# Expert gate and up weights in tiles of their own, one product each, and an unused product beside the routing: a two-block network on one Trainium2 core

## The chip, the cores and the metric

The kernel runs on one NeuronCore of a Trainium2 chip. The metric is the device time of one execution in microseconds (us). The engines are PE (TensorE; its weight loads are shown apart, as PEld), DVE (VectorE), ACT (ScalarE), POOL (GpSimd) and SP (SyncE, which here issues nearly all loads). An L with a number, such as L1540, is a line of the kernel.

## The reference

Two blocks are computed one after the other on 256 tokens of width 1024, all in float32: a recurrent and sliding-window block with an MLP, then a block with latent attention, pooling, attention to a memory, and a mixture of experts. The change lies in the mixture of experts, which ends the program:

```python
group_prob = softmax(xn @ w_rg + b_rg); g_w, g_idx = top_k(group_prob, 1)
sel = (the 8 expert logits of the chosen group)
e_w, e_idx = top_k(softmax(sel), 2)
cw = (g_w * renormalised e_w, spread over the 32 experts)
for e in range(32):
    hid = silu(xn @ w_gate[e]) * (xn @ w_up[e])       # 1024 x 256 each
    out = out + (hid * cw[:, e:e+1]) @ w_down[e]      # 256 x 1024
x = rms_norm(x + out, final_norm_g)
```

Each token goes to 2 of 32 experts, but all experts' weights are read: 32 x 3 matrices of 1 MB.

## The kernel before

The program is written in the order in which each engine is to do its work; that order is kept. Loads go out on SP's queue in one fixed list (`raws`), each as soon as a slot for it is free. A **raw** is 1 MB of weights. There are ten big slots (7 and 3), and up to eight small ones, each made of two half-size activation tiles (`rawa`).

**The experts' rounds.** After the routing the experts are put in order of their load and worked through in ten rounds: four wide rounds of two experts with 64 token slots each, then six rounds of four experts with 32 slots each. Two rounds make a batch. In a round the experts stand side by side: expert i's products write the output partitions from 64i (or 32i), so that their products run at the same time on different columns of the array. The first six experts have fixed numbers, so their 18 raws can be loaded before the routing is known and fill all 18 slots; later ones are looked up (`ids`).

**One expert's weights.** `load_gu` (L1438) fills one raw with half of the 1024 rows of gate and of up: four rows to a partition (runs of 4 KB in DRAM), gate in one half of the tile and up in the other, two DMAs. In a small slot the same takes four DMAs with runs of 2 KB. `load_d` (L1447) loads the down matrix in runs of 8 KB, or of 4 KB in a small slot. `gu` (L1533) multiplies: for each of four k of a half, one product of 512 columns gives gate and up at once (L1540). `first` (L1588) does this for the first half, `second` (L1604) for the second half and then the activation; `down` (L1597) transposes the hidden values, multiplies by the down matrix and adds the result of the round before to the output (`scatter`).

**The routing.** `after_x(c)` (L1066) runs when half c of the block's residual x is done: it transposes x for the logits (L1091), sums squares (L363, into the place of the split), and copies x into `xs[t][0]` on ACT (L1097). `fours` (L1101) is the order of these copies: four neighbouring columns of x are put 128 apart, so that tile k of the transposed x fits the weights' rows. `split_rest` (L1106) takes the remainder of that split on DVE (L1109). `prepare0` (L1520) then runs, in this order: `residual(0)` (L1573; a product with the identity that puts x into the output's accumulators, L1578), `route` (L1282, a chain of small DVE steps from L1291 to L1318, then five small PE products from L1321), `onehots(0)` (L1470, L1474), `places` (the experts' order), `gather(0, ...)` for k 0 to 3 (L1482: each k takes four products on PE, L1490, and a copy with the norm's gain on ACT, L1493), `split_rest(1)`, and `weights` (DVE steps up to `cws`, L280). The first round's `first` follows, and in it the other four gathers, `slots_of(0)` (L1494, which reads `cws`) and `residual(1)`. For later batches `second` runs the gathers of the next batch, four before its products and four after the activation.

Of the kernel before, what the change touches and what calls it, by code (L numbers as in the profile page):

```python
# [10 lines left out]
F32 = mybir.dt.float32  # L11
# [10 lines left out]
P = 128  # L22
# [77 lines left out]
class Net:  # L100
# [965 lines left out]
    def after_x(self, c):  # L1066
# [13 lines left out]
        sq = lambda t: self.sumsq(self.X[t][:, cs], 512, self.xs[t][0][:, cs])  # L1080
# [25 lines left out]
    def split_rest(self, c):  # L1106
        cs = slice(c * 512, (c + 1) * 512)
        for t in range(2):
            self.nc.vector.tensor_sub(self.fours(self.xs[t][1], c), self.X[t][:, cs],  # L1109
                                      self.fours(self.xs[t][0], c).bitcast(F32))  # L1110
# [134 lines left out]
    def setup3(self):  # L1245
# [12 lines left out]
        for n, d in ((slice(0, 4), slice(0, 4)), (slice(4, 36), slice(8, 40))):  # L1258
            nc.gpsimd.tensor_tensor(self.wr[:, :, d], w[:, :, n], g.to_broadcast([P, 8, n.stop - n.start]), op=ALU.mult)
            nc.gpsimd.tensor_copy(self.br[:, d], self.free[:, o + n.start:o + n.stop])  # L1260
        self.tri = cp.tile([P, P], BF16, name="tri")
# [20 lines left out]
    def route(self):  # L1282
# [36 lines left out]
        s2 = sel01.rearrange("p t g e -> p t (g e)")  # L1319
        p = self.pt((P, 3, E))  # L1320
# [4 lines left out]
        nc.tensor.matmul(p[:, 2, :], self.ones, s2[:, 1, :], start=False, stop=True)  # L1325
        self.pm = self.cp.tile([P, 2, E], F32, name="pm")
# [91 lines left out]
    def moe(self):  # L1418
# [38 lines left out]
        def gu_of(raw, k):  # L1457

            x = raw[k * len(raw) // 4].rearrange("p a b -> p (a b)").rearrange("p (j k n) -> p j k n", j=2, n=256)
            return x[:, :, k % (4 // len(raw)), :]  # L1460
# [21 lines left out]
        def gather(b, kts):  # L1482
            for k in kts:
# [9 lines left out]
                nc.scalar.mul(xg[b, k // 4][:, k % 4, :], p, self.col("ffn_cols", k, 1))  # L1493
# [26 lines left out]
        def prepare0():  # L1520
            self.small_slots = 16
            self._loads()
            residual(0)
# [251 lines left out]
```

## Time and profile before

| what | value |
|---|---|
| median of 3 runs | 966.74 us (965.71 to 968.67) |
| the profiled execution | 966.64 us, its span 964.9 us |
[...]
| PE busy / DVE / ACT | 904.4 / 547.6 / 472.5 us |
| bytes read from DRAM | 220.59 MB, 230 GB/s over the span |

The page also cuts the span into 40 slices of 24 us. These lines give, for each slice, the granted TensorE clock and the busy share of PE and of the DMA engines in tenths, and the GB/s that they moved:

```profile
PE   6999999999999999999999999999998999857775
PEclk9999999999999999999999999999997999879768
DMA  9644244586365555454665444356678999999994
GB/s 292 212 142 172 89 132 148 170 292 209 95 217 201 193 184 200 162 178 134 208 212 171 176 156 153 132 177 212 246 267 320 370 406 400 389 409 409 406 406 185
```

Such lines are read by stage: a digit of 9 tells which resource is full there. [...]

### The profile page before, as it was taken

To read this page: it belongs to the slowest core of one execution; us is meant where nothing else is said; L and a number is where in the kernel's file an instruction comes from. 1 tells how busy PE (TensorE), PEld (TensorE's weight loads), DVE (VectorE), ACT (ScalarE), POOL (GpSimd) and SP (SyncE) were. 2 spreads that over 40 slices of the span, in tenths; PEclk is the share of its full clock that TensorE was granted. 3 is DMA by queue.
4 is the path that set the end of the run, shared out by engine and by line. 5 is a ranking of instruction groups with operands and counts; after the bars stand their busy time and mean duration, and the time that the engine had idled before them with its cause. 6 is when DMAs were issued, how large, how long until landed. Compare 5 with 4: busy or idle time off the path is not lost.

```text
span 964.9 us, 14222 instructions
## 1 busy us (share of the span) xinstructions
PE 904.4 (94%) x5265; PEld 700.6 (73%) x5265; DVE 547.6 (57%) x1101; ACT 472.5 (49%) x900; POOL 34.6 (4%) x71
## 2 busy tenths in 40 slices
PE   6999999999999999999999999999998999857775
PEld 5889898888899999988988787999884444313212
DVE  5986889776675555567756558856447222201002
ACT  5666779754655454456665645645542322102002
POOL 4200000000000000000200000000000000000000
PEclk9999999999999999999999999999997999879768
DMA  9644244586365555454665444356678999999994
GB/s 292 212 142 172 89 132 148 170 292 209 95 217 201 193 184 200 162 178 134 208 212 171 176 156 153 132 177 212 246 267 320 370 406 400 389 409 409 406 406 185
DMA packets 97783, 222.63 MB, mean 231 GB/s; under 512 B 9378, under 2 KB 13739, under 8 KB 96427
## 3 DMA queue, kind: packets, MB, share of 16 engines
q1 hardware_dynamic: 94016, 218.91, 63.7%
q10 hardware_dynamic: 3691, 2.74, 0.9%
q8 instruction: 43, 0.70, 0.3%
q14 instruction: 33, 0.27, 0.1%
HBM read 220.59 MB, written 1.05 MB: 230 GB/s over the span
## 4 chain that ended last, share of the span: by engine, by line
PE 79%; DMA 14%; DVE 3%; issue 2%; ACT 1%; SPq 1%; POOL 0%; DVEq 0%; ACTq 0%; POOLq 0%
PE acc L313 18%; PE acc L315 18%; PE acc L314 18%; PE pt L1540 5%; DMA raw<-in_w_exp_gate_dram 4%; DMA rawa<-in_w_exp_down_dram 4%; PE pt L314 3%; PE pt L315 3%; PE pt L313 3%; DMA raw<-in_w_exp_up_dram 2%; DMA rawa<-in_w_exp_gate_dram 2%; PE pt L1562 2%; PE pt L286 1%; PE pt L1490 1%; DMA raw<-in_w_exp_down_dram 1%
## 5 line engine op out<-in xcount | busy, mean ns | idle before, releaser
L280 DVE TENSOR_TENSOR w<-raw,w 128x512 fp32r<-128x512 f32 (+4 forms) x288 | 273.5, 968 | 117.8 <-ACT w L279 115.9
L279 ACT CAST w<-raw 128x512 fp32r<-128x512 f32 (+4 forms) x288 | 236.4, 847 | 153.7 <-PE acc L315 117.8
L313 PE MATMUL acc<-w,st 128*128 128x512 f32 (+2 forms) x508 | 197.7, 392 | 0.0
L314 PE MATMUL acc<-w,st 128*128 128x512 f32 (+2 forms) x508 | 197.4, 389 | 0.0
L315 PE MATMUL acc<-w,st 128*128 128x512 f32 (+2 forms) x508 | 193.3, 389 | 0.2 <-DVE w L280 0.2
L1540 PE MATMUL pt<-raw,xg 128*32 128x512 f32 (+1 forms) x360 | 97.4, 698 | 31.3 <-DMA raw<-in_w_exp_up_dram 31.3
L315 PEld LDWEIGHTS acc<-w,st 128*128 128x128 f32 x508 | 95.8, 189 | 19.1 <-DVE w L280 0.6
L313 PEld LDWEIGHTS acc<-w,st 128*128 128x128 f32 x508 | 95.9, 189 | 18.4 <-ACT st L279 0.5
L314 PEld LDWEIGHTS acc<-w,st 128*128 128x128 f32 x508 | 96.0, 189 | 17.6 <-DVE st L280 0.2
L1540 PEld LDWEIGHTS pt<-raw,xg 128*32 128x32 f32 (+1 forms) x360 | 22.6, 131 | 86.8 <-issue 82.4
L280 DVE TENSOR_TENSOR y<-pt,y 128x512 fp32r<-128x512 f32 x20 | 13.8, 692 | 123.4 <-ACT y L279 123.4
L314 PE MATMUL pt<-st,w 128*128 128x256 f32 x256 | 73.1, 286 | 1.8 <-DVE w L280 1.8
L315 PE MATMUL acc<-st,w 128*128 128x256 f32 x256 | 73.7, 288 | 0.0
L313 PE MATMUL acc<-st,w 128*128 128x256 f32 x256 | 73.5, 287 | 0.0
L314 PE MATMUL acc<-st,w 128*128 128x256 f32 x256 | 73.4, 287 | 0.0
L313 PE MATMUL pt<-st,w 128*128 128x256 f32 x256 | 73.0, 286 | 0.0
L315 PE MATMUL pt<-st,w 128*128 128x256 f32 x256 | 72.5, 286 | 0.0
L314 PEld LDWEIGHTS pt<-st,w 128*128 128x128 f32 x256 | 49.9, 195 | 2.2 <-DVE w L280 2.0
L313 PE MATMUL acc<-w,hid 128*128 128x512 f32 x128 | 50.0, 390 | 0.0
L313 PEld LDWEIGHTS pt<-st,w 128*128 128x128 f32 x256 | 49.8, 195 | 0.2
L314 PE MATMUL acc<-w,hid 128*128 128x512 f32 x128 | 49.9, 390 | 0.0
L315 PE MATMUL acc<-w,hid 128*128 128x512 f32 x128 | 49.8, 389 | 0.0
(393 smaller groups left out, 1346.4 us busy)
## 6 DMA issues: line engine op xcount, KB each, us to landing
raw<-in_w_in_dram SPq DMA_DIRECT2D x31, 1024.0 KB, 5.2
raw<-in_w_exp_gate_dram SPq DMA_DIRECT2D x45, 512.0 KB, 7.0
raw<-in_w_exp_up_dram SPq DMA_DIRECT2D x45, 512.0 KB, 8.0
rawa<-in_w_exp_down_dram SPq DMA_DIRECT2D x44, 512.0 KB, 8.7
raw<-in_w_up_dram SPq DMA_DIRECT2D x16, 1024.0 KB, 5.6
raw<-in_w_down_dram SPq DMA_DIRECT2D x16, 1024.0 KB, 6.2
raw<-in_w_exp_down_dram SPq DMA_DIRECT2D x10, 1024.0 KB, 10.0
rawa<-in_w_exp_gate_dram SPq DMA_DIRECT2D x38, 256.0 KB, 7.5
```

Of the source, the lines that this page charges most:

```text
L279: self.nc.scalar.copy(h, src)
L280: self.nc.vector.tensor_sub(l, src, h.bitcast(F32))
L286: self.nc.tensor.transpose(p[:, i, :], src[:, i * P:(i + 1) * P], self.ident)
L313: mm(acc, xh, wh, start=start, stop=False)
L314: mm(acc, xl, wh, start=False, stop=False)
L315: mm(acc, xh, wl, start=False, stop=stop)
L1490: nc.tensor.matmul(p, xs[t][i][:, k * P:(k + 1) * P], oh[b, t], start=n == 0, stop=n == 3)
L1540: nc.tensor.matmul(guP[p][q].rearrange("s (j f) -> s j f", j=2), xg[b, hf][:, k, j * P + q.start:j * P + q.stop], gu_of(x, k), start=kt == ...
L1562: nc.tensor.matmul(q[s], hT[p][:, f, s], d_of(x, f, c), start=f == 0, stop=f == 1)
```

## The change

`load_m` replaces `load_gu`: a raw now holds one whole matrix of an expert, gate or up, with eight rows to a partition, in one DMA (two in a small slot). `first` multiplies by gate alone and `second` by up alone, each with eight products of 256 columns. The order of x's columns follows (`eights` in place of `fours`, and the gain `g8`, loaded by a small DMA on ACT's queue). All eight gathers are now needed before `first`. The remainder of x's second half is taken in two parts: for tokens 0 to 127 at the end of `after_x(1)`, for the others after `onehots(0)`. `keep` issues products into an accumulator that is overwritten later: ten ahead of the routing's PE products and four behind them. The four accumulators are taken at the start of `prepare0`. (A path for overfull experts, which does not run with these inputs, changes likewise.)

```diff
@@ after_x
-        sq = lambda t: self.sumsq(self.X[t][:, cs], 512, self.xs[t][0][:, cs])
+        sq = lambda t: self.sumsq(self.X[t][:, cs], 512)
...
         for t in range(2):
-            nc.scalar.copy(self.fours(self.xs[t][0], c), self.X[t][:, cs])
-        if c == 0:
-            self.split_rest(0)
+            nc.scalar.copy(self.eights(self.xs[t][0], c), self.X[t][:, cs].rearrange("q (p k) -> q p k", k=8))
+        for t in range(2 - c):
+            self.split_rest(c, t)
-    def fours(self, x, c):
-        return x[:, c * 512:(c + 1) * 512].rearrange("q (k p) -> q p k", k=4)
+    def eights(self, x, c):
+        return x.rearrange("q (k p) -> q p k", k=8)[:, c * 64:(c + 1) * 64, :]
...
+    def keep(self, acc, n):
+        for _ in range(n):
+            self.nc.tensor.matmul(acc, self.identr, self.eights(self.xs[0][0], 0), start=True, stop=True)
@@ setup3
+        self.g8 = cp.tile([P, 8], F32, name="g8")
...
+        nc.scalar.dma_start(self.g8, rows.rearrange("(p k) -> p k", k=8))
@@ route
+        self.keep(self.acc[0, 1], 10)
         p = self.pt((P, 3, E))
         nc.tensor.matmul(p[:, 0, :], self.tri, s2[:, 0, :], start=True, stop=True)
...
         nc.tensor.matmul(p[:, 2, :], self.ones, s2[:, 1, :], start=False, stop=True)
+        self.keep(self.acc[0, 1], 4)
@@ moe
-        def load_gu(e, hf):
+        def load_m(e, w):
             def f(parts):
-                n = 4 // len(parts) * 256
+                rows = e.of(w).rearrange("(p k) n -> p (k n)", k=8)
+                n = 2048 // len(parts)
                 for i, x in enumerate(parts):
-                    for j, w in enumerate((wg, wu)):
-                        rows = e.of(w)[hf * 512:(hf + 1) * 512, :].rearrange("(p k) n -> p (k n)", k=4)
-                        runs = x.rearrange("p a b -> p (a b)")
-                        nc.sync.dma_start(runs[:, j * n:(j + 1) * n], rows[:, i * n:(i + 1) * n])
+                    nc.sync.dma_start(x.rearrange("p a b -> p (a b)"), rows[:, i * n:(i + 1) * n])
...
         def prepare0():
...
+            for t in range(2):
+                for c in range(2):
+                    acc[t, c] = self.accp()
             residual(0)
             places, weights = self.route()
             onehots(0)
+            self.split_rest(1, 1)
             places()
-            gather(0, range(4))
-            self.split_rest(1)
+            gather(0, range(8))
             weights()
...
-        def gu(p, hf, tiles):
+        def gu(p, i, tiles):
...
-            for k in range(4):
-                kt = 4 * hf + k
+            for k in range(8):
                 for x, q in zip(tiles, own(p)):
-                    nc.tensor.matmul(guP[p][q].rearrange("s (j f) -> s j f", j=2),
-                                     xg[b, hf][:, k, j * P + q.start:j * P + q.stop], gu_of(x, k), start=kt == 0,
-                                     stop=kt == 7)
+                    nc.tensor.matmul(guP[p][q, i * 256:(i + 1) * 256],
+                                     xg[b, k // 4][:, k % 4, j * P + q.start:j * P + q.stop], m_of(x, k), start=k == 0,
+                                     stop=k == 7)
...
-        gus = [[[load_gu(e, hf) for e in of_round(p)] for hf in range(2)] for p in range(NP)]
+        gus = [[[load_m(e, w) for e in of_round(p)] for w in (wg, wu)] for p in range(NP)]
...
             if p == 0:
-                gather(0, range(4, 8))
                 slots_of(0)
                 residual(1)
...
         def second(p, tiles):
             b, j = divmod(p, 2)
-            if b < NB - 1 and j:
-                gather(b + 1, range(4))
             gu(p, 1, tiles)
             act(p)
             if b < NB - 1 and j:
-                gather(b + 1, range(4, 8))
+                gather(b + 1, range(8))
                 slots_of(b + 1)
```

## Rows read from the trace of the kernel before

**Rows 1.** Stretches: us, PE, PEld, DVE, ACT, POOL busy, PEclk, DMA share, GB/s.

```profile
725.00:730.00 5.00, 1.59 (x11) 1.26 (x11) 4.17 (x23) 0.00 (x0) 0.00 (x0) 0.77 0.99 356
735.00:740.00 5.00, 5.00 (x19) 1.61 (x16) 4.26 (x29) 0.25 (x1) 0.00 (x0) 0.70 0.61 245
740.00:745.00 5.00, 5.00 (x34) 3.56 (x34) 2.72 (x13) 2.43 (x5) 0.00 (x0) 1.00 0.84 297
745.00:750.00 5.00, 5.00 (x26) 1.72 (x24) 1.13 (x3) 0.47 (x1) 0.00 (x0) 1.00 0.61 211
750.00:950.00 200.00, 166.25 (x958) 64.39 (x954) 32.06 (x92) 36.04 (x73) 0.00 (x0) 0.87 1.02 400
```

**Rows 2.** The chain that ended last, at its end: start, us, what.

```profile
939.88 10.12 DMA rawa<-in_w_exp_down_dram
950.04 2.76 PE pt L1562 x18
```

**Rows 3.** Gate's DMA issues from 739 to 950 us (up's are as many).

```profile
raw<-in_w_exp_gate_dram SPq DMA_DIRECT2D x37, 512.0 KB, 9.0
...
rawa<-in_w_exp_gate_dram SPq DMA_DIRECT2D x30, 256.0 KB, 7.5
```

**Rows 4.** Timeline of SP's issues, 820 to 835 us; one, five and one left out.

```profile
820.29 0.33 SPq L1445 DMA_DIRECT2D raw<-in_w_exp_up_dram  x1
...
825.27 0.33 SPq L1445 DMA_DIRECT2D rawa<-in_w_exp_up_dram  x1
...
832.96 0.33 SPq L1445 DMA_DIRECT2D rawa<-in_w_exp_up_dram  x1
...
834.32 0.33 SPq L1445 DMA_DIRECT2D rawa<-in_w_exp_up_dram  x1
```

**Rows 5.** Timeline of SP's issues, 728 to 748 us.

```profile
729.10 2.36 SPq L1454 DMA_DIRECT2D rawa<-in_w_exp_down_dram  x4
739.73 0.36 SPq L1445 DMA_DIRECT2D raw<-in_w_exp_gate_dram  x1
...
747.40 0.34 SPq L1445 DMA_DIRECT2D raw<-in_w_exp_gate_dram  x1
```

**Rows 6.** The chain that ended last, through the first round.

```profile
734.27 5.42 PE pt L1540 x16
739.70 2.11 PE pt L1490 x16
741.81 0.37 PE pt L1500 x4
...
742.66 1.13 PE acc L1578 x4
743.79 7.02 PE pt L1540 x32
```

**Rows 7.** Timeline of ACT, DVE and PE through the routing.

```profile
722.33 1.97 ACT L1097 CAST xs<-x 128x512 fp32r<-128x512 f32 x2
...
723.97 0.43 DVE L1291 SCALAR_TENSOR_TENSOR lg<-pt,rf,br 128x40 f32<-128x40 f32 x2 [0.81 <-POOL rf L1095]
...
727.80 0.21 PE L1321 MATMUL pt<-sel,tri 128*128 128x32 bf16 x1 [2.54 <-DVE sel L1318]
...
728.41 0.76 DVE L1474 TENSOR_TENSOR oh<-pm,slots 128x256 fp32r<-128x256 f32 x2
...
728.98 2.90 PE L1490 MATMUL pt<-oh,xs 128*128 128x256 f32 x12 [0.86 <-DVE oh L1474]
...
731.40 1.99 DVE L1109 TENSOR_TENSOR xs<-x,xs 128x512 fp32r<-128x512 f32 x2
...
739.19 0.23 DVE L280 TENSOR_TENSOR cws<-hw,cws 128x66 fp32r<-128x66 f32 x1 [0.31 <-ACT cws L279]
```

**Rows 8.** Chain: float32 products of 256 columns; then L1540's weight loads, 743 to 800 us.

```profile
688.77 3.45 PE pt L1046 x16
...
L1540 PEld LDWEIGHTS pt<-raw,xg x88: 106/137/137, 743.7 to 798.4; 128*64 128x64 f32 x72, 128*32 128x32 f32 x16
```

More of the change, by code (lines that the diff above doesn't have):

```diff
@@ L1096, in after_x, with split_rest @@
         for t in range(2):
-            nc.scalar.copy(self.fours(self.xs[t][0], c), self.X[t][:, cs])
-        if c == 0:
-            self.split_rest(0)
-    def fours(self, x, c):
-        return x[:, c * 512:(c + 1) * 512].rearrange("q (k p) -> q p k", k=4)
-    def split_rest(self, c):
-        cs = slice(c * 512, (c + 1) * 512)
-        for t in range(2):
-            self.nc.vector.tensor_sub(self.fours(self.xs[t][1], c), self.X[t][:, cs],
-                                      self.fours(self.xs[t][0], c).bitcast(F32))
+            nc.scalar.copy(self.eights(self.xs[t][0], c), self.X[t][:, cs].rearrange("q (p k) -> q p k", k=8))
[3 more added lines that the diff above has]
+        return x.rearrange("q (k p) -> q p k", k=8)[:, c * 64:(c + 1) * 64, :]
+    def split_rest(self, c, t):
+        cs = slice(c * 512, (c + 1) * 512)
+        self.nc.vector.tensor_sub(self.eights(self.xs[t][1], c), self.X[t][:, cs].rearrange("q (p k) -> q p k", k=8),
+                                  self.eights(self.xs[t][0], c).bitcast(F32))
+    def keep(self, acc, n):
+        for _ in range(n):
+            self.nc.tensor.matmul(acc, self.identr, self.eights(self.xs[0][0], 0), start=True, stop=True)
     def mla_lat(self, t, lat, klat, kr, st_q, st_kv):
@@ L1260, in setup3 @@
             nc.gpsimd.tensor_copy(self.br[:, d], self.free[:, o + n.start:o + n.stop])
+        self.g8 = cp.tile([P, 8], F32, name="g8")
+        o, n = ROW["ffn_norm_g_2"]
+        rows = self.a["rows"][o:o + n, :].rearrange("r n -> (r n)")
+        nc.scalar.dma_start(self.g8, rows.rearrange("(p k) -> p k", k=8))
         self.tri = cp.tile([P, P], BF16, name="tri")
@@ L1456, in moe, with m_of @@
         xs = self.xs
-        def gu_of(raw, k):
-            x = raw[k * len(raw) // 4].rearrange("p a b -> p (a b)").rearrange("p (j k n) -> p j k n", j=2, n=256)
-            return x[:, :, k % (4 // len(raw)), :]
+        def m_of(raw, k):
+            n = 8 // len(raw)
+            return raw[k // n].rearrange("p a b -> p (a b)")[:, k % n * 256:(k % n + 1) * 256]
         d_of = lambda raw, f, c: raw[0][:, 2 * f + c, :] if len(raw) == 1 else raw[f][:, c, :]
@@ L1492, in gather @@
                         n += 1
-                nc.scalar.mul(xg[b, k // 4][:, k % 4, :], p, self.col("ffn_cols", k, 1))
+                nc.scalar.mul(xg[b, k // 4][:, k % 4, :], p, self.g8[:, k:k + 1])
         def slots_of(b):
@@ L1575, in residual @@
             for t in range(2):
-                acc[t, c] = self.accp()
                 for i in range(2):
-                    nc.tensor.matmul(acc[t, c], self.identr, self.fours(xs[t][i], c), start=i == 0,
+                    nc.tensor.matmul(acc[t, c], self.identr, self.eights(xs[t][i], c), start=i == 0,
                                      stop=False)
         self.ids = None
-        gus = [[[load_gu(e, hf) for e in of_round(p)] for hf in range(2)] for p in range(NP)]
+        gus = [[[load_m(e, w) for e in of_round(p)] for w in (wg, wu)] for p in range(NP)]
         ds = [[load_d(e) for e in of_round(p)] for p in range(NP)]
@@ L1690, in overflow @@
                     x = self.big([P, 8, 256], F32, "wo")
-                    for c in range(2):
-                        rows = a[n][0, e, c * 512:(c + 1) * 512, :]
-                        nc.sync.dma_start(x[:, 4 * c:4 * c + 4, :], rows.rearrange("(p k) n -> p k n", k=4))
+                    nc.sync.dma_start(x, a[n][0, e].rearrange("(p k) n -> p k n", k=8))
                     w.append(x)
```

4 lines of the change are left out of this document (2 added, 2 removed).

## The prediction

> **What bounds the kernel now.** I read the page's slices first: DMA stands at 9 from slice 29 on, while PE's digits fall. Cutting that part into stretches shows it best: from 750 to 950 us the DMA share is 1.02 and 400 GB/s flow, while PE is busy 166 of 200 us, much of it at the lower clock [rows 1]. The chain agrees: its last long piece is the DMA of a down matrix, and 14.9 us (964.9 - 950.0) of products, norm and output follow it [rows 2]. So the end is: when the experts' stream runs without a gap, plus its bytes over its rate, plus a tail that the change doesn't touch. Two things can move it.
>
> First, **the gap ahead of the stream**. The 18 preloaded raws fill every slot, and SP's last issue before the gap is followed by none until 739.73 [rows 5], when the first products (end 739.70) free two slots [rows 6]. From 735 to 750 us only (245 + 297 + 211) x 5 = 3.77 MB flow; at 400 GB/s that is 9.4 us of work, so 5.6 us are lost [rows 1]. By the same count data stop at 735 + 3.1 = 738.1 and start again at 745 - 3.7 = 741.3, 1.6 us after the issue.
>
> Second, **the rate**. In rows 4 SP issues one DMA each time an earlier one lands, so its spacing is their time. Two 1 MB down DMAs with 8 KB runs took 825.27 - 820.29, 2.49 us each; six of 512 KB with 4 KB runs took 7.69 us, 2.56 us per MB; two of 256 KB with 2 KB runs took 1.36 us, 2.72 us per MB [rows 4].
>
> **The change, part by part.** *Longer runs.* From 739 us on gate is issued 37 times at 512 KB and 30 times at 256 KB, up as often [rows 3]: that is 37 raws in big slots (one DMA each of gate and up) and 15 in small ones (two each). Big ones go from 4 to 8 KB runs and save 0.07 us each, small ones from 2 to 4 KB and save 0.16 us. The first two are big and fall into the gap; 35 x 0.07 + 15 x 0.16 = 4.9 us. Ends: 0, if memory gives no more, and 8.0 us, if every raw gained what the small ones do (50 x 0.16). I take 4.9, since the 8 KB rows were taken in the same saturated stretch.
>
> *The routing.* The remainder for tokens 0 to 127 now stands on DVE ahead of L1291. It needs the first of ACT's two copies (722.33 plus half of 1.97, about 723.4) and takes half of 1.99, so DVE is free at 724.4 instead of 723.97: +0.45 us, the rest lies in DVE's 0.81 us wait for POOL [rows 7]. Everything up to the small PE products (727.80) moves by that, to 728.25. Behind the one-hots (728.41 to 729.17, now 729.6) the other remainder takes 1.0 us, to 730.6, and the first gather's fourth product waits for it; the experts' order comes 1.45 us later, but no slot is free for a looked-up expert before 738, so that costs nothing unless the first products free one before the order is known, about 733.
>
> *The unused products.* PE is free at 727.80 - 2.54 = 725.26 [rows 7]. An identity product over the strided copy took 1.13 / 4 = 0.28 us at full clock [rows 6], so ten end at 728.1, before the small products are due, and the four behind them at 729.4, when the one-hots arrive (728.98 + 0.45). They cover the idle time and delay nothing; at half clock the ten would take 5.7 us and push the routing back by 2.7. [...]
>
> *The first round.* Before, four gathers, half the products, four gathers, slots, residual, the other half. Now eight gathers: 730.6 + 0.13 + 7 x 0.53 = 734.5, against 734.27 before, for twice the work. ACT's copies keep up, at less than a gather each. Then gate: 734.5 + 3.5 = 738.0; the first slots come free 1.7 us earlier. `slots_of(0)` needs `cws`, ready at 739.4 before [rows 7]; DVE reaches `weights` some 0.3 us earlier, since the two remainders (1.99 us) stood ahead of it and 1.45 us have come in elsewhere. So PE waits from 738.0 to 739.1, then takes 743.79 - 741.81 = 2.0 us as before and 3.5 us for up: 744.6 against 743.79 + 3.51 = 747.3. The second pair of slots is issued at 744.7 instead of 747.40 [rows 5]. The two raws loaded meanwhile end at 738.1 + 1.6 + 2 x 2.5 = 744.7, before the new data can arrive (746.3), so this second restart decides: the stream is **2.7 us** earlier. Ends: 0 (the clock falls all the same) and 5.6 (no gap left).
>
> *One product for each matrix.* Twice as many products of half the columns. The nearest row is a float32 stream with 256 columns and loads of 128: 16 records in 3.45 us, 0.216 each [rows 8], against 0.219 for half of a 512-column record pair (7.02 / 32) [rows 6]. Cost 0; the loads (137 ns at most [rows 8]) are hidden by records of 216 ns. If that cover fails, see the third rival.
>
> *Pacing.* Until about 800 us PE sets how fast slots come free, and it starts 2.7 us earlier, no more. What longer runs save in these rounds, about 22 raws' share (1.4 us), is partly lost. Ends 0 and 1.4; I take 0.5.
>
> *At nothing:* half as many issues (SP waits for landings anyway [rows 4]); the gain's small DMA (one issue on ACT's queue, far from the end); the later batches' gathers, all behind the up products (the same work, in rounds where PE waits for data or is serial anyway); the accumulators taken early (DVE has read their old contents before L1291); the squares' own tile (same instruction).
>
> **Sum:** 2.7 + 4.9 - 0.5 = 7.1 us. The profiled execution took 966.64 us, 0.10 below the median of the runs: 966.6 - 7.1 = **959.5 us**.
>
> **The rivals.** *1. The unused products don't hold the clock.* Two idle stretches stay (0.8 us before the second remainder, 1.1 us before `cws`). If the clock falls at 729 all the same, eight gathers take 730.6 + 0.2 + 7 x 0.97 = 737.6, gate 5.42 (743.0), then 2.0 and 3.5: 748.5, 1.2 us later than before. With 4.9 from the stream and the whole 1.4 of pacing lost: 966.6 + 1.2 - 3.5 = 964.3 us. Against it: the clock was 1.00 from 740 to 750 us with such waits in it [rows 1].
>
> *2. Longer runs bring nothing*, because something shared is full at 400 to 410 GB/s. For it: the saturated stretch is flat. Against it: the 8 KB rows, at 1.049 MB / 2.49 us = 421 GB/s [rows 4]. Then only the gap shrinks: 966.6 - 2.7 = 963.9 us. [...]
>
> *3. Slower: weight loads are no longer hidden.* The two experts of a round use the same array rows and different columns. If a load had to wait for the products in flight, each of 32 steps of a wide round (8 k, two records, two matrices) would cost 0.137 us more, 4.4 us a round, 17.5 us over four. Less the 2.7 us of the start, the slots come free 14.8 us later when the narrow rounds begin; some 55 raws then save 3.6: 966.6 + 14.8 - 3.6 = 977.8 us. It decides from about 60 ns a step (7.7 us). In narrow rounds the same is hidden by the stream. Against it: the 128-column loads of rows 8 hide under products of the same length. [...]
>
> *4. No gap left.* If PE gets ahead enough that the stream never stops, 5.6 + 4.9: 956.1 us.
>
> **How the numbers follow.** Forecast 0.62, rival 1 0.10, rival 2 0.10, rival 3 0.08, rival 4 0.10. A measurement of this kernel can tell about 0.3%, 2.9 us, so faster means below 963.8 us. The forecast, rival 4, and two fifths to three fifths of rivals 1 and 2 (both lie on that line, and each may hold in part) give 0.82 faster, 0.10 the same, 0.08 slower. The range goes from 955.5, just under rival 4, to 964.5, past rivals 1 and 2; it leaves out rival 3 and about as much again for what I haven't thought of.
>
> **What would show it.** Right: the granted clock at 1.00 from 725 to 745 us; the small products at 728 and not later; gate's first products at about 734.5, some 3.5 us long; SP's first looked-up issue near 738 and its third near 744.7; SP's spacing in the saturated part 2.5 us for 1 MB of gate or up, 1.28 us for 512 KB; 410 GB/s or more from 750 us on. Wrong: L1540's successors with more than 0.23 us a record; a DMA share under 0.95 between 755 and 800 us (PE's pace); 1 MB landing every 2.56 us.

## The result and the profile after

The changed kernel took **961.64 us** (median of 11 runs, 960.31 to 965.43), the kernel before beside it 967.46 us (11 runs, 964.21 to 969.45): a ratio of 0.995, 95% interval 0.9934 to 0.9966, about 4.8 us less by the ratio and 5.8 us by the medians. The forecast was 7.1 us less. The profiled execution of the changed kernel took 960.31 us, its span is 958.6 us, its granted clock 0.971 (in the profile of the kernel before 0.964).

First the stretches of the changed kernel, with the columns of [rows 1].

```profile
725.00:730.00 5.00, 5.00 (x16) 1.97 (x15) 1.83 (x7) 0.00 (x0) 0.00 (x0) 1.00 1.00 370
735.00:740.00 5.00, 4.10 (x39) 2.78 (x36) 4.26 (x29) 0.47 (x4) 0.00 (x0) 1.00 0.24 54
740.00:745.00 5.00, 5.00 (x34) 2.62 (x34) 2.51 (x11) 0.59 (x1) 0.00 (x0) 1.00 0.88 365
745.00:750.00 5.00, 4.61 (x42) 2.80 (x38) 0.90 (x2) 0.78 (x2) 0.00 (x0) 1.00 0.73 243
750.00:800.00 50.00, 49.88 (x386) 30.55 (x388) 13.05 (x40) 14.90 (x31) 0.00 (x0) 1.00 1.01 407
800.00:900.00 100.00, 75.14 (x750) 38.42 (x750) 14.42 (x44) 16.86 (x34) 0.00 (x0) 0.85 1.02 414
```

And the last two of these stretches in the kernel before:

```profile
750.00:800.00 50.00, 49.19 (x270) 23.26 (x267) 13.05 (x40) 14.81 (x31) 0.00 (x0) 1.00 1.03 398
800.00:900.00 100.00, 79.09 (x472) 29.52 (x474) 14.43 (x44) 16.81 (x34) 0.00 (x0) 0.84 1.02 403
```

Three things stand here. The clock is 1.00 from 725 to 750 us, where before it was 0.77 and 0.70 [rows 1]: read by half microseconds, before has it at 1.00 until 727.5 us, at 0.50 from 728 to 737.5, and at 1.00 again from 738. The stream is faster: 414 GB/s for 403. But the gap ahead of it has not shrunk: from 735 to 750 us (54 + 365 + 243) x 5 = 3.31 MB flow, at 407 GB/s worth 8.1 us, so 6.9 us are lost where the kernel before lost 5.6.

The DMA issues of the stream (738 to 950 us) against [rows 3]: as many bytes, 67 issues for gate and up, where gate alone had that many.

```profile
raw<-in_w_exp_gate_dram SPq DMA_DIRECT2D x20, 1024.0 KB, 13.8
raw<-in_w_exp_up_dram SPq DMA_DIRECT2D x17, 1024.0 KB, 10.8
rawa<-in_w_exp_up_dram SPq DMA_DIRECT2D x18, 512.0 KB, 14.4
rawa<-in_w_exp_gate_dram SPq DMA_DIRECT2D x12, 512.0 KB, 9.4
```

SP's issues in the saturated part, as [rows 4] read for the kernel before: four issues of up from 816.59 us, then two from 826.63.

```profile
816.59 7.88 SPq L1456 DMA_DIRECT2D rawa<-in_w_exp_up_dram  x4
826.63 2.81 SPq L1456 DMA_DIRECT2D raw<-in_w_exp_up_dram  x2
```

Each of these waits for a 1 MB transfer with 8 KB runs ahead of it to land: four steps in 826.63 - 816.59 us are 2.51 us each, as forecast, where 4 KB runs had 2.56.

So it is the other half of the forecast, the start, that has to be looked at. The chain that ended last shows where. The first columns are start and length in us.

```profile
721.47 2.09 PE acc L1590 x4
723.55 4.92 PE acc L1115 x10
...
740.15 1.96 PE acc L1590 x4
742.11 7.06 PE pt L1553 x64
...
933.27 10.02 DMA rawa<-in_w_exp_down_dram
```

The ten unused products (L1115) are on the chain: 4.92 us, 0.49 us each, though the clock was at 1.00. The same product over the old order took 0.28 us [rows 6]. The residual's products (L1590), which the change did not mean to touch, went from 1.13 to 1.96 us as well. The timeline of DVE, PE and SP's queue gives the consequence.

```profile
725.36 0.22 DVE L1328 TENSOR_TENSOR sel<-s 128x64 bf16<-128x64 f32 x1
728.30 0.21 PE L1332 MATMUL pt<-sel,tri 128*128 128x32 bf16 x1
728.65 0.23 DVE L1339 SCALAR_TENSOR_TENSOR pm<-sel,pt 128x64 f32<-128x64 bf16 x1 [3.06 <-PE pt L1336]
734.45 3.67 PE L1553 MATMUL pt<-raw,xg 128*64 128x256 f32 x32
738.15 1.54 SPq L1456 DMA_DIRECT2D raw<-in_w_exp_gate_dram  x2
739.03 0.63 PE L1511 MATMUL pt<-cws,oh 128*128 128x66 f32 x4 [0.90 <-DVE cws L280]
745.74 0.34 SPq L1456 DMA_DIRECT2D raw<-in_w_exp_up_dram  x1
```

DVE had the routing's selection done at 725.58 us; PE took it at 728.30, behind the unused products, and DVE sat idle for 3.06 us (before: PE waited for DVE, 2.54 us [rows 7]). Everything that waits for it moved by 2.7 us.

To compare runs, whose routing starts at different times, the following table counts from the start of the first logits step on DVE (L1291 before, L1301 after), by the timeline's rows: the routing's first small product, the first products with an expert's weights, the first and the third raw that SP issues after the gap, the last landing of an expert's weights, and the end of the span.

| profiled execution | small product | first gate | first raw | third raw | last landing | end |
|---|---|---|---|---|---|---|
| before | 3.83 | 10.24 | 15.76 | 23.43 | 226.02 | 240.89 |
| before_again | 3.84 | 10.23 | 15.86 | 23.53 | 228.70 | 243.4 |
| after | 6.50 | 12.65 | 16.35 | 23.94 | 221.50 | 236.81 |
| keep_plain | 3.91 | 9.94 | 13.63 | 21.33 | 218.99 | 234.35 |
| keep_plain_2 | 5.29 | 11.31 | 15.01 | 24.01 | 221.62 | 236.79 |
| no_keep | 3.83 | 10.94 | 14.64 | 21.29 | 219.30 | 234.67 |
| fours_whole | 3.83 | 9.01 | 12.70 | 21.79 | 223.57 | 238.46 |
| short_runs | 6.50 | 12.65 | 16.35 | 23.92 | 230.65 | 246.66 |
| late_slots | 5.24 | 11.26 | 14.95 | 18.41 | 219.35 | 234.42 |
| late_residual | 3.83 | 9.84 | 13.54 | 16.99 | 216.45 | 231.73 |
| late_residual_no_keep | 3.83 | 10.92 | 14.62 | 18.07 | 217.68 | 232.90 |

The experts' part thus became 226.02 - 221.50 = 4.5 us shorter to the last landing, although its first raw is asked for 0.6 us later. (The profiled executions themselves are 6.3 us apart; 2.2 us of that lie ahead of the routing, see before_again.)

Two things limit what the table can tell. First, before and before_again are the same kernel, and their last landings are 2.7 us apart; so a difference of that size between two single profiles proves little, and the readings below lean on marks that several profiles share. The steadiest of them is the time from the third raw to the last landing: 197.6, 197.7, 197.6 and 198.0 us in after, keep_plain, keep_plain_2 and no_keep, against 202.6 and 205.2 us in the two profiles of the kernel before. Second, the count starts behind a step that the change itself delays:

```profile
720.65 0.70 POOL L1095 TENSOR_TENSOR rf<-s,mhalf 128x2 f32<-128x2 f32 x1 [103.77 <-DVE s L1092]
721.80 0.42 DVE L1301 SCALAR_TENSOR_TENSOR lg<-pt,rf,br 128x40 f32<-128x40 f32 x2
```

The logits start 721.80 - 721.35 = 0.45 us after POOL's `rf` in the changed kernel, as forecast, where the kernel before has 0.03 us (723.97 against 723.24 + 0.70). Counted from POOL's step, each gain on the kernel before is 0.4 us smaller.

### The profile page after: what moved, and what is told of

Read it like the earlier page. It is cut to its first block, busy times and chain, and to the rows that moved or that the text cites. A ratio compares the mean times of both kernels' runs of the same rounds, so it can differ in the third digit from the quotient of the medians.

```text
span 958.6 us, 14980 instructions
## 1 busy us (share of the span) xinstructions
PE 896.1 (93%) x5791; PEld 720.1 (75%) x5791; DVE 547.7 (57%) x1101; ACT 473.2 (49%) x900; POOL 34.5 (4%) x71
## 4 chain that ended last, share of the span: by engine, by line
PE 82%; DMA 11%; DVE 3%; issue 1%; ACT 1%; POOL 0%; SPq 0%; DVEq 0%; POOLq 0%; ACTq 0%
PE acc L313 18%; PE acc L315 18%; PE acc L314 18%; PE pt L1553 6%; DMA raw<-in_w_exp_gate_dram 5%; PE pt L314 3%; PE pt L315 3%; PE pt L313 3%; PE pt L1575 3%; DMA rawa<-in_w_exp_down_dram 2%; DMA rawa<-in_w_exp_up_dram 2%; DMA raw<-in_w_exp_down_dram 1%; PE pt L286 1%; PE acc L1584 1%; PE pt L1501 1%
## 5 line engine op out<-in xcount | busy, mean ns | idle before, releaser
L1553 PE MATMUL pt<-raw,xg 128*32 128x256 f32 (+1 forms) x720 | 86.0, 427 | 37.1 <-DMA raw<-in_w_exp_gate_dram 37.1
L1553 PEld LDWEIGHTS pt<-raw,xg 128*32 128x32 f32 (+1 forms) x720 | 41.7, 129 | 70.2 <-issue 30.7
L314 PEld LDWEIGHTS pt<-st,w 128*128 128x128 f32 x256 | 49.1, 192 | 2.3 <-DVE w L280 2.0
L313 PEld LDWEIGHTS acc<-st,w 128*128 128x128 f32 x256 | 49.0, 191 | 0.7 <-issue 0.4
```

The lines of the kernel that those rows point to most:

```text
L313: mm(acc, xh, wh, start=start, stop=False)
L314: mm(acc, xl, wh, start=False, stop=False)
L1553: nc.tensor.matmul(guP[p][q, i * 256:(i + 1) * 256], xg[b, k // 4][:, k % 4, j * P + q.start:j * P + q.stop], m_of(x, k), start=k == 0, st ...
```

## Experiments

Unless said otherwise a kernel is the changed kernel with the edit shown, and each ratio is to runs of the kernel before beside it, whose medians were 964.7 to 965.1 us. Beside the changed kernel it was 967.46 us, so kernels are compared by their ratios.

### The unused products: without them, and over neighbouring columns

no_keep drops both calls:

```diff
-        self.keep(self.acc[0, 1], 10)
...
-        self.keep(self.acc[0, 1], 4)
```

> The changed kernel without its fourteen unused products, all else as changed. Theory A (the products read the new order of x at 0.49 us each instead of the 0.28 I forecast, so the ten hold the routing's small products from about 725.6 until 728.3): without them the routing is 2.9 us shorter; if the granted clock stays at 1.00 through 725 to 740 us, 958.7 us. Rival B (the clock is worth more than the products cost): the clock falls to its lower level during the gathers and the first gate products, gathers near 7.8 us in place of 4.0 and gate 5.4 in place of 3.5, so the second pair of slots comes free some 2 us later: 963.4 us.

keep_plain leaves them in, but lets them read 512 neighbouring columns instead of the strided view:

```diff
-            self.nc.tensor.matmul(acc, self.identr, self.eights(self.xs[0][0], 0), start=True, stop=True)
+            self.nc.tensor.matmul(acc, self.identr, self.xs[0][0][:, 0:512], start=True, stop=True)
```

> The changed kernel, but the fourteen unused products read 512 neighbouring columns instead of the new order. Theory A: 0.23 us each, ten take 2.3 us and end when the routing's products are due; clock still 1.00; first looked-up load 2.5 to 2.9 us sooner after the routing's start than in the changed kernel, and 958.9 us. Rival B (the time of the products is hidden or regained later by the stream): as the changed kernel, 961.6 us within 1 us.

Measured: no_keep 958.65 us, ratio 0.9928 [0.9909, 0.9948]; keep_plain 959.95 us, 0.9937 [0.9917, 0.9957]. By the ratios, leaving out the strided products gains 2.1 us on the changed kernel and replacing them 1.3 us (0.3 in a second series, below), with intervals that overlap the changed kernel's (0.9934 to 0.9966); no_keep's 958.7 us was forecast for a clock that stays at 1.00, which it did not (below). What the totals can't settle, the timeline of keep_plain does:

```profile
723.38 2.50 PE L1115 MATMUL acc<-xs,identr 128*128 128x512 f32 x10
725.73 0.19 PE L1332 MATMUL pt<-sel,tri 128*128 128x32 bf16 x1
```

Ten products now take 2.3 us by the chain, 0.23 each, and the small product is back at 3.91 us after the logits. To the last landing this execution gains 226.02 - 218.99 = 7.0 us on the kernel before, 6.6 counted from POOL's step: **near the forecast's 7.1, once the unused products cost what they were priced at.** It is one execution of a faster kind, as the second profile shows (below); by its two ratios keep_plain gains 5.1 to 6.1 us.

In no_keep the clock falls; the row is its stretch from 725 to 730 us:

```profile
725.00:730.00 5.00, 2.91 (x15) 2.55 (x16) 4.23 (x20) 0.62 (x2) 0.00 (x0) 0.50 0.99 358
```

Its first gate products come 1.0 us later than in keep_plain, but its third raw at the same time (21.29 and 21.33), since PE waits for `cws` before up in both. What quicker unused products bring to this kernel is therefore next to nothing, and the strided ones cost it time.

keep_plain was run a second time, beside fours_whole (below).

> The same kernel as keep_plain, beside fours_whole on one chip: 959 to 960 us, 850 to 900 us near 418 GB/s.

Measured: 960.40 us, 0.9947 [0.9933, 0.9961]. Its profiled execution (961.23 us) differs from the first (957.88 us) in two places. The first fence is the stretch from 724 to 728 us in keep_plain, the second the same in keep_plain_2 and its stretch from 740 to 745 us (1.00 in keep_plain), the third two rows of its timeline, the fourth one of its chain.

```profile
724.00:728.00 4.00, 3.58 (x21) 2.47 (x19) 3.40 (x16) 0.00 (x0) 0.00 (x0) 1.00 0.98 372
```

```profile
724.00:728.00 4.00, 4.00 (x13) 2.77 (x12) 2.23 (x14) 0.00 (x0) 0.00 (x0) 0.59 0.99 334
740.00:745.00 5.00, 5.00 (x24) 2.37 (x24) 2.17 (x9) 0.39 (x1) 0.00 (x0) 0.66 0.86 351
```

```profile
724.23 3.87 PE L1115 MATMUL acc<-xs,identr 128*128 128x512 f32 x10
...
727.94 0.19 PE L1332 MATMUL pt<-sel,tri 128*128 128x32 bf16 x1
```

```profile
741.73 8.36 PE pt L1553 x64
```

With PE busy throughout, the clock still fell to its lower level for a part of the unused products; they ran into the small products' time and made them 1.4 us later (5.29 against 3.91). Behind PE's wait for `cws` it fell a second time, and the products of up and of the next gate took 8.36 us where they take 7.06 at 1.00: another 1.3 us. Together that puts the third raw at 24.01 and the last landing at 221.62, by chance where the changed kernel has them. The twelve runs of keep_plain fall into two groups, four from 957.4 to 957.9 us and eight from 959.8 to 961.2, and the two profiles are one of each. Over the whole span the granted clock is 0.970 to 0.972 in the four and 0.966 to 0.970 in the eight, which fits; where the unprofiled runs lost it was not seen.

### The runs in DRAM: shorter again, in two ways

short_runs cuts each load of gate or up along its run, into two DMAs of half the run length; nothing else changes.

```diff
-                    nc.sync.dma_start(x.rearrange("p a b -> p (a b)"), rows[:, i * n:(i + 1) * n])
+                    x = x.rearrange("p a b -> p (a b)")
+                    for j in range(2):
+                        nc.sync.dma_start(x[:, j * n // 2:(j + 1) * n // 2],
+                                          rows[:, i * n + j * n // 2:i * n + (j + 1) * n // 2])
```

> The changed kernel, but each load of gate or up is cut into two DMAs along the run: 4 KB runs in big slots and 2 KB runs in small ones, as before the change. Bytes, order and tiles are the same. Theory A (longer runs bring the stream some 5 us): 966 to 967 us, GB/s from 800 to 900 us back near 405. Rival C (what the stream gained came from elsewhere, such as fewer issues or the later gathers): as the changed kernel, 961.6 us.

Measured: 967.75 us, ratio 1.0024 [1.001, 1.0038]. That is 0.74% more than the changed kernel's ratio, some 7 us, and more than the 4.9 forecast for the runs. Stretches:

```profile
750.00:800.00 50.00, 50.00 (x388) 30.50 (x386) 13.05 (x40) 15.41 (x31) 0.00 (x0) 1.00 1.02 388
800.00:900.00 100.00, 72.58 (x718) 37.64 (x718) 14.42 (x44) 15.89 (x32) 0.00 (x0) 0.81 1.03 402
```

From 800 us on the rate is that of the kernel before (403); from 750 to 800 it is lower than before's 398. But the edit changes two things, the length of the runs and the number of DMAs, so it can't say which. fours_whole parts them: it takes keep_plain, puts x back into blocks of four columns, and fetches a matrix with the old run lengths, in as few DMAs as the changed kernel.

```diff
-        return x.rearrange("q (k p) -> q p k", k=8)[:, c * 64:(c + 1) * 64, :]
+        return x[:, c * 512:(c + 1) * 512].rearrange("q (k p) -> q p k", k=4)
...
-                rows = e.of(w).rearrange("(p k) n -> p (k n)", k=8)
-                n = 2048 // len(parts)
+                rows = e.of(w).rearrange("(c p k) n -> p c (k n)", c=2, k=4)
+                n = 1024 // len(parts)
                 for i, x in enumerate(parts):
-                    nc.sync.dma_start(x.rearrange("p a b -> p (a b)"), rows[:, i * n:(i + 1) * n])
+                    nc.sync.dma_start(x.rearrange("p a b -> p (a b)").rearrange("p (c m) -> p c m", c=2),
+                                      rows[:, :, i * n:(i + 1) * n])
```

> keep_plain with the row order of the kernel before: x in blocks of four columns, and each gate or up matrix fetched with runs of 4 KB (2 KB in a small slot), but still as one DMA per matrix (two in a small slot), one product each, unused products over neighbouring columns. So the run lengths go back, the number of DMAs does not. Theory R (the length of the runs is the whole gain of the stream): 750 to 800 us near 395 GB/s and 850 to 900 near 409, the time 959.9 + 7.1 from the cut loads - 0.8 for the quicker residual products = 966 us, about the kernel before. Theory P (the pieces of a run lying 8 KB apart in DRAM, as in the cut loads, cost the last 2 us, the run length the 4.9 of the prediction): 959.9 + 4.9 - 0.8 = 964 us, 850 to 900 us near 412. Theory C (the number of DMAs counts, not the run length): 959 us, 418 GB/s.

Measured: 960.09 us, 0.9953 [0.994, 0.9966]: as fast as keep_plain beside it, which by the totals alone speaks for the number of DMAs. The stretches say otherwise (two rows of fours_whole, then one of keep_plain):

```profile
750.00:800.00 50.00, 50.00 (x387) 30.39 (x384) 13.74 (x41) 15.44 (x32) 0.00 (x0) 1.00 1.03 404
800.00:900.00 100.00, 74.26 (x732) 37.78 (x736) 13.74 (x43) 16.21 (x33) 0.00 (x0) 0.83 1.03 405
```

```profile
800.00:900.00 100.00, 77.05 (x760) 39.53 (x759) 14.44 (x44) 16.34 (x34) 0.00 (x0) 0.83 1.02 413
```

405 GB/s with 4 and 2 KB runs in few DMAs and much the same in twice as many (402 in short_runs, 403 before, 404 in before_keep), and 413 or 414 with 8 and 4 KB runs (keep_plain, both times, and the changed kernel): **the rate follows the run length.** Over the 180 us or so of full stream that is 180 x (1 - 405/414) = 3.9 us; from profile to profile, fours_whole's last landing is 4.6 us behind keep_plain's, of which its third raw has 0.5, so 4.1. The totals show less of it: four of its five runs lie from 959.8 to 960.3 us (the profiled one, 962.01 us, is its slowest), while eight of keep_plain's twelve lie 2 to 3 us above the other four. From lowest run to lowest run the difference is 2.4 us. So the runs are worth 2.4 to 4.1 us; the times of theories R and P were too high, the rates of R came true.

fours_whole is also the change without longer runs: its last landing is 226.02 - 223.57 = 2.5 us ahead of the kernel before's, where the start was forecast at 2.7. That they are so close is in part luck: its third raw is only 23.43 - 21.79 = 1.6 us earlier, and against before_again its landing is 5.1 us earlier.

What short_runs loses beyond 4 us lies in part between 750 and 800 us (388 against 404 GB/s in 50 us are 0.8 MB, 2 us) and was not followed further. Besides having more DMAs than fours_whole, it takes from DRAM pieces that lie 8 KB apart (theory P); which of the two costs this was not told apart.

half_dmas was meant to part the two in another way: two DMAs with unchanged runs, each over 64 partitions.

```diff
+                    for q in (slice(0, 64), slice(64, P)):
-                    nc.sync.dma_start(x.rearrange("p a b -> p (a b)"), rows[:, i * n:(i + 1) * n])
+                        nc.sync.dma_start(x.rearrange("p a b -> p (a b)")[q], rows[q, i * n:(i + 1) * n])
```

> The changed kernel, but each load of gate or up is issued as two DMAs of 64 partitions each: as many DMAs as before the change (178 of experts' weights after the routing instead of 111), with the changed kernel's runs of 8 and 4 KB. The run without the longer runs was some 7 us slower than the changed kernel, where spacing of landings gave 5. Theory A (run length alone): as the changed kernel, 961 us within 1. Rival E (the number of DMAs counts too, since SP keeps only a few in flight and small ones leave it short): 2 us or more slower, 963 us or above.

Measured: 1089.47 us, 1.1196 [1.1139, 1.1253], outside theory A, and so far beyond rival E that something else must act. Its stretch from 800 to 900 us:

```profile
800.00:900.00 100.00, 55.20 (x436) 27.36 (x440) 7.96 (x24) 8.79 (x18) 0.00 (x0) 0.74 1.02 268
```

The DMA share is 1.02 with 268 GB/s: the engines were busy and slow. This run says nothing on the number of DMAs, but something on partitions: see the last section.

### The order of x's columns

natural keeps x in its own order, so that identity products read neighbouring columns, and lets the gathers' weight loads take every eighth column instead:

```diff
-        return x.rearrange("q (k p) -> q p k", k=8)[:, c * 64:(c + 1) * 64, :]
+        return x[:, c * 512:(c + 1) * 512]
...
-                        nc.tensor.matmul(p, xs[t][i][:, k * P:(k + 1) * P], oh[b, t],
+                        nc.tensor.matmul(p, xs[t][i].rearrange("q (p k) -> q k p", k=8)[:, k, :], oh[b, t],
```

> The changed kernel, but xs keeps x's own order: the copies, the remainders, the identity products and the unused products read and write neighbouring columns, and the gathers' weight loads pick every eighth column instead. Theory A: identity products 0.23 us, copies and remainders shorter by 0.3 us each, the second residual 1 us shorter, so 1 to 1.5 us better than with plain unused products alone: 957.5 us. Rival D (a weight load over every eighth column is slower): the gathers' 0.13 us a product grows to 0.2 or more, the first eight gathers take 6 us or more instead of 4.0, and the gain is lost: 960 to 963 us.

Measured: 965.21 us, 0.9999 [0.9987, 1.001], slower than either theory had it. Two rows of its chain, with the eight gathers of the first batch, and those of the second batch in keep_plain's:

```profile
726.32 7.94 PE pt L1501 x32
...
738.92 0.92 PE acc L1590 x4
```

```profile
754.64 4.03 PE pt L1501 x32
```

The residual's products are at 0.23 us, but 32 gather products take 7.94 us, against 4.03 in keep_plain. With five batches of gathers on PE, the order of the changed kernel is the better one.

### The unused products in the order of before

before_keep adds `keep` (the ten and the four) to the kernel before, over its own strided copy, at 0.28 us or less, and takes the accumulators early.

> The kernel before, with the unused products alone added (ten ahead of the routing's products, four behind, in the old order of x, where they cost 0.28 us), and the accumulators taken early. Theory A: the clock stays at 1.00 from 725 to 745 us, the first four gathers and the first half of the products save some 2 to 2.5 us, the first looked-up load is issued that much earlier, but the gap behind it stays; 1.5 to 2.5 us faster than before, 962.5 to 963.5 us. Rival F (as in the changed kernel with or without plain unused products, the later wait for the slots' weights takes it back): as before within 1 us.

Measured: 965.80 us, 1.0008 [0.9994, 1.0021]: nothing. The stretches of its routing:

```profile
725.00:730.00 5.00, 2.69 (x19) 2.23 (x17) 4.69 (x20) 0.99 (x3) 0.00 (x0) 1.00 1.06 404
730.00:735.00 5.00, 5.00 (x19) 1.53 (x17) 4.56 (x27) 0.88 (x4) 0.00 (x0) 0.66 0.89 353
```

and one row of its timeline:

```profile
729.01 1.78 ACT L1499 ACTIVATE xg<-pt,cols 128x256 f32<-128x256 f32 x4 [8.33 <-DVE xs L1113]
```

The clock holds to 730 us and falls behind it: ACT's copies of the gathers wait for DVE's second remainder (they read nothing of it; that its source holds the buffer that they write is argued from the program, not shown), PE waits for ACT, and the first products (16 in 5.35 us by the timeline) run no faster than in [rows 6]. In the old order the unused products gained nothing that lasted: that kernel's last landing, 226.13 us after the logits, is the kernel before's (226.02).

before_again is the kernel before once more, in a single execution.

> The kernel before, once more, for its profile: in the one profile of before the routing starts (first step on the logits) at 724.0 us, in five profiles of kernels with the change at 720.9 to 722.2. Theory A (start-up scatter, nothing of the change lies ahead of that point but a small DMA): somewhere from 721 to 724 us. Rival H (the change shortens the time ahead of the routing): 724 us again.

Measured: 968.76 us. The logits of before_again and of before_keep:

```profile
723.60 0.43 DVE L1291 SCALAR_TENSOR_TENSOR lg<-pt,rf,br 128x40 f32<-128x40 f32 x2 [0.81 <-POOL rf L1095]
```

```profile
720.36 0.43 DVE L1295 SCALAR_TENSOR_TENSOR lg<-pt,rf,br 128x40 f32<-128x40 f32 x2 [0.82 <-POOL rf L1095]
```

They start at 723.60 us; in the kernel before they started at 723.97, in before_keep, where nothing on DVE or POOL ahead of them differs, at 720.36. The time ahead of the routing thus scatters by over 3 us, and the 2.2 us by which the changed kernel's logits are earlier (721.80) can't be put down to the change. The other profiles of kernels with the new order have 720.9 to 722.7; whether that is more than chance stays open.

### The second restart, and PE's pace

The forecast had it that the third raw's issue, when up's first products end, decides when the stream runs. late_slots is keep_plain with `slots_of(0)`, which waits for `cws`, and `residual(1)` moved behind those products.

```diff
...
-            if p == 0:
-                slots_of(0)
-                residual(1)
...
+            if p == 0:
+                slots_of(0)
             act(p)
+            if p == 0:
+                residual(1)
```

> The changed kernel with plain unused products, and with the slots' weights and the second residual moved behind the first round's up products. In the run with plain unused products alone PE waits for the weights' DVE chain and then takes some 3 us ahead of up. Theory A (the second pair of free slots sets where the stream restarts): the third looked-up load comes some 4 us earlier after the routing's start, 17.2 us in place of 21.3, the gap from 735 to 750 us shrinks by 2.5 us or more, 957 us. Rival G (PE's pace in the wide rounds sets the stream, and the work moved is only paid later): as with plain unused products alone, 959 to 960 us.

Measured: 958.55 us, 0.9927 [0.9906, 0.9947], lowest 955.99; by the totals alone it can't be told from keep_plain. In its profiled execution the clock fell in the unused products as in keep_plain_2 (0.50 from 724 to 726 us in both, first gate at 11.26 and 11.31), so that is the one to compare. SP's queue, late_slots:

```profile
736.61 1.55 SPq L1456 DMA_DIRECT2D raw<-in_w_exp_gate_dram  x2
740.07 0.34 SPq L1456 DMA_DIRECT2D raw<-in_w_exp_up_dram  x1
```

The third raw goes out 5.6 us earlier (18.41 against 24.01 after the logits); 1.3 us of that are keep_plain_2's second fall of the clock, which late_slots doesn't have (1.00 from 740 to 745 us), and 4.3 us the move itself. The last landing comes 2.3 us earlier. More than half is lost again on the way, and the chain of waits lies on PE until about 800 us, where PE is busy 50.00 of 50 us. So a second thing sets the start: how much work PE has in the wide rounds.

late_residual tests that: late_slots, with all eight residual products (x into the accumulators) in the seventh round, where PE waits for data, and the first down products starting the accumulators; 16 unused products ahead of the routing's small ones, to fill the place.

```diff
-        self.keep(self.acc[0, 1], 10)
+        self.keep(self.acc[0, 1], 16)
...
-            residual(0)
...
-                        nc.tensor.matmul(acc[t, c], stt[b][:, j, t, :], y[p, c][i], start=False,
+                        nc.tensor.matmul(acc[t, c], stt[b][:, j, t, :], y[p, c][i], start=p == 0 and i == 0,
...
+            if p == 6:
+                for c in range(2):
+                    residual(c)
```

> As the run with late slots' weights, and the eight residual products (0.49 us each) moved out of the first round into the seventh, where PE waits for data; the first addition into each accumulator starts it instead. Sixteen plain unused products ahead of the routing's products in place of ten, since the first residual's no longer stand there. Theory G (until about 800 us PE's pace, not the second restart, sets the stream): PE reaches the second round's up products 2 us sooner after the routing's start than with late slots' weights alone, and the whole is 1.5 to 2 us faster than that, 956.5 to 957 us. Rival I (the stream is at its own rate already): as with late slots' weights, 958.5 us.

late_residual_no_keep is the same without unused products.

> The same without any unused product, and so with PE idle for some 4 us ahead of the routing's products. Theory A: the clock falls there and in the first gathers, which costs 1 to 2.5 us of PE's head start against the run with sixteen products: 958 to 959 us. Rival J (PE is warm again in time, as in the changed kernel without unused products, where they made no difference that could be told): the same time as with them.

Measured: **late_residual 954.93 us (954.55 to 955.41), 0.9893 [0.9877, 0.9909]**, some 10 us less than the kernel before and 5 to 6 less than the changed one; without unused products 957.02 us (956.04 to 957.61), 0.9913 [0.9898, 0.9928]. Stretches, the first two rows of late_residual:

```profile
725.00:730.00 5.00, 4.17 (x31) 3.60 (x32) 4.24 (x21) 1.89 (x4) 0.00 (x0) 1.00 1.01 384
...
750.00:800.00 50.00, 50.00 (x418) 30.63 (x418) 13.05 (x40) 14.83 (x30) 0.00 (x0) 1.00 1.01 412
```

and one of late_residual_no_keep:

```profile
725.00:730.00 5.00, 2.98 (x16) 2.61 (x17) 4.22 (x20) 0.69 (x2) 0.00 (x0) 0.50 1.01 384
```

Both are some 1 to 2 us faster than expected. PE is still full to 800 us, and gets through 418 records there where keep_plain has 387. Against no_keep, with the same clock (0.50 from 725 to 730 us in both), the last landing is 1.6 us earlier (217.68 for 219.30): that is the two moves. Now the unused products are worth 2.1 us by the medians, and the runs of the two don't overlap. In the profiles 1.2 us of it (216.45 for 217.68) lie behind the logits: PE no longer waits for `cws` between gate and up, so what it gains in the gathers is kept.

## Why the prediction was right and where it was not

**Direction and range: right, the mechanism by half.** 961.64 us lies in the range, 2.1 us above the forecast. Of the two named causes the stream came true and the earlier start did not; the range was wide enough to hold that. Some of the signs came true by luck: the small products at 728.30 us, gate at 734.45, the first issue at 738.15 stand where they were forecast (728, 734.5, 738) only because this execution reached its logits at 721.80 us and not at 724.4; after the logits the small products are 2.7 us late.

**Longer runs, 4.9 us: the price was right, the sum a little high.** 1 MB took 2.51 us, where the down matrices had 2.49 [rows 4]. fours_whole puts the whole at 2.4 to 4.1 us. The time from the third raw to the last landing is 4.1 us shorter in keep_plain than in fours_whole (197.7 for 201.8), and 5 us or more shorter than in the kernel before. Rival 2 (nothing) is out: the stream ran at 414 GB/s, where the kernel before had 403.

**The start, 2.7 us: the step that failed is the price of the unused products.** "An identity product over the strided copy took 1.13 / 4 = 0.28 us at full clock" was taken from a row of the old order and applied to the new one. The change itself altered what these products read: where four neighbours of x lay 128 columns apart, now eight do, and the product takes 0.49 us. Ten of them end 2.7 us after the routing's selection is ready, and "delay nothing" became 2.7 us, besides 0.8 us in `residual(1)` between gate and up. In place of 2.7 us earlier, the third raw came 0.5 us later (23.94 against 23.43). The prediction had even worked out that number, 2.7 us, for the case of half the clock: it looked at the clock and not at the form of the operand. Without that error the third raw comes 1.6 us earlier in fours_whole and 2.1 in keep_plain.

**The clock: right.** It was 1.00 from 725 to 745 us in the changed kernel, so rival 1 did not happen there, though for the wrong reason in part: the products were twice as long, and PE had no idle time left. With products of 0.23 us the clock fell during or just ahead of them in two of five profiles (0.50 from 724 to 726 us in keep_plain_2 and late_slots, 1.00 from 720 to 730 us in keep_plain, fours_whole and late_residual), and behind the wait for `cws`, as rival 1 feared, in keep_plain_2 and fours_whole (0.66 from 740 to 745 us, 0.67 from 735 to 740). What the forecast held against it, a clock of 1.00 from 740 to 750 us "with such waits in it", was misread: PE was busy 5.00 of 5 us in both of those stretches [rows 1]. What the forecast took for a k of the gathers and for gate are times at two clocks: 0.53 us (16 products in 2.11) and 3.51 (half of 7.02) at 1.00 [rows 6], and 0.97 (12 products in 2.90 [rows 7]) and 5.42 us [rows 6] at 0.50, which for gate held until 737.5 us. At 1.00 the changed kernel's 32 gather products took 4.01 us, 0.50 a k, and gate 3.67.

**"This second restart decides": half right.** Issued 5.6 us earlier in late_slots, it gave 2.3; PE's pace in the wide rounds takes the rest. What that pace costs the changed kernel itself, for which the forecast took 0.5 us, no run measures. Rival 4 (no gap left) is out: 6.9 us of the gap stayed.

**One product for each matrix, 0: right.** 64 records of 256 columns took 7.06 us, the 32 of 512 columns 7.02 [rows 6]. Rival 3 (loads not hidden, 977.8 us) is out: with these weights of 128x64 on different columns a pair of records took 0.22 us (7.06 / 32), where loads that wait would have made it 0.36 (an estimate, with the 0.137 us more of [rows 8]).

**At nothing: right for the DMAs' number from 800 us on** (403 and 404 GB/s with many, in before and before_keep, 405 with few, in fours_whole; open for short_runs ahead of that), **wrong for the residual's products**, which the forecast left at what they took before: the same misread operand.

The gain of the changed kernel, by its profiles: 4 to 5 us from the stream, less 0.5 us of later start. What is left open is what lies ahead of the routing: there the kernels with the change lie from 720.9 to 722.7 us, and three profiles of the old order scatter by 3.6.

## What to carry to other kernels

When a change reorders data, price every instruction that reads it anew: a duration carries over only with its access pattern (0.23, 0.28 and 0.49 us here for one and the same product), and a row of the old order is no evidence for the new. Filler work must end well before the instruction that it stands ahead of, at the slower clock too; otherwise it turns from cover into a wait (2.7 us in the changed kernel, 1.4 in keep_plain_2), and it pays only where the time that it saves is not spent at the next wait (2.1 us in late_residual, next to nothing in keep_plain). When the totals of two kernels agree, compare the rates and marks inside the profile before concluding that an edit did nothing: here a stream of 413 GB/s for 405 did not show in the totals (960.40 us for keep_plain_2, 960.09 for fours_whole), and the profile of keep_plain_2 has the clock at 0.59 from 724 to 728 us.

A sign of being right that is given as a time from the start of the program can come true by chance; give it from the last step ahead of the change.

## What the runs showed that was not expected

- **A strided moving operand slows a product at a clock of 1.00.** Per 512 columns: 0.23 us over neighbouring columns (keep_plain, natural), 0.28 us where four neighbours in a row lie 128 columns apart [rows 6], 0.49 us where eight do. No run here tells why eight cost more than four.
- **Weight loads over every eighth column** nearly doubled the gather: 7.94 us for 32 products (natural) against 4.03 (keep_plain), both at a clock of 1.00.
- **DMAs over 64 partitions are much slower**, also when the two halves of a tile are fetched one after the other with several in flight (512 KB of gate landed 17.9 us after its issue, in the median): 268 GB/s at a DMA share of 1.02, where the changed kernel has 414. If the down matrices, a third of the bytes and still fetched to all partitions, went at 414, gate and up went at some 228 GB/s (an estimate from these two rates). No run here tells why.
- **The run length still counts at 4 KB**: 405 GB/s with 4 and 2 KB runs of gate and up, 413 or 414 with 8 and 4 KB, at a DMA share of 1.02 or 1.03 in both.
- **The clock fell while PE was busy.** In keep_plain_2 the granted clock was 0.59 from 724 to 728 us with PE busy 4.00 of 4 us, in keep_plain, the same program, 1.00. In 741 to 744 us it stood at 0.50, with PE busy 3.00 of 3 us and a wait of 1.00 us some two us earlier; keep_plain, with the same wait, had 1.00.
